# Two edits to the order of work in a hybrid attention block: pinned splits of the mixed heads, and six filling steps ahead of each first score

## The chip, the core and the metric

The kernel runs on one core of one Trainium2 chip. Its metric is the device time of one execution, in microseconds (us). TensorE (PE in the profile) multiplies; VectorE (DVE) and ScalarE (ACT) work on its results and prepare its operands; GpSimd (POOL) issues some of the DMA transfers, SyncE (SP) most of the others. Each engine takes its instructions in the order of its own program and waits at the first whose inputs or buffers are not ready.

## What is computed

One residual block on a sequence of 512 tokens of 2048 columns, in float32:

```python
def hybrid_layer(x, cos, sin, pre_norm_w, w_in, q_norm_w, w_q_up, kv_norm_w, w_kv_up, w_out, post_norm_w):
    h = rms_norm(x, pre_norm_w)
    sb_q, sb_k, sb_v, sb_gate, c_q, c_kv, k_rope, mla_gate = jnp.split(h @ w_in, split_pts, axis=-1)
    o_a = from_heads(stick_breaking_attention(to_heads(sb_q, 8), to_heads(sb_k, 8), to_heads(sb_v, 8)))
    ...
    o_b = from_heads(chunk_causal_softmax_attention(q_mla, k_mla, v_mla.transpose(0, 2, 1, 3)))
    mixed = jnp.concatenate([o_a * jax.nn.silu(sb_gate), o_b * jax.nn.silu(mla_gate)], axis=-1)
    y = mixed @ w_out
    return x + rms_norm(y, post_norm_w)
```

Both attentions have 8 heads of 128 columns. In the stick-breaking one a score row goes through two sigmoids, a running product from the right, and a multiplication; the row that comes out weighs the values.

## The kernel before

**Products in three parts.** Every float32 operand is split into a high part (an ACT copy to the float32r type, line 96) and a low part (a DVE subtraction, line 99), by `split`. A product is three matmuls (`mm3`, line 127): high by high, high by low, low by high. A tile is 128 partitions by 512 columns unless it says otherwise.

**Two streams on TensorE.** Ahead of the attention and inside it, one generator, `filler` (line 635), yields the large products one step at a time; a step is one `mm3`, three matmuls of 512 columns for nearly all. In its order: the rest of the input projection, the gates of the softmax heads, then for each stick-breaking head `q`, `k` and `gate` (16 steps each; and ahead of heads 0 and 4 the values of four heads, 64 steps), then two column groups of the output product (`out_group`, 64 steps each), then the last columns. `fill(n)` takes n steps. The attention of the heads is written between such calls, so that TensorE has a filling step to do while ACT and DVE work on a head.

**A stick-breaking head** (lines 921 to 954) takes steps until its `k` and `q` are there (`need`), then `fill(4)`, then for each block b of 128 queries the scores `z` (one `mm3`; 256, 256, 384 and 512 columns), the mask, the sigmoids, the product, and 1, 3, 3 and 7 filling steps; then for each of four blocks of keys the transposes `tp`, their split `th`/`tl`, `fill(3)`, and the product with the values, `av`. The gated result `mix` goes to DRAM (`mixed[i]`, line 794, on POOL's queue). Ahead of the scores `k` is scaled (`kr`, DVE) and split (`kh` on ACT, `kl` on DVE).

**The mixed heads.** The output product needs the 16 mixed heads split again. `split_mixed` (line 381) loads one from DRAM (`mx`, POOL's queue, line 392) and splits it into `mxh` and `mxl`; `out_group(0)` calls it four times at its start and then once for each of the 16 products of 128 rows (line 447). Its order is the softmax heads 8 to 15, then 0 to 7. Later, `load_pair` and `first_sums` (lines 486 to 500) load the mixed heads again in eight pairs, one pair for each of eight pieces of weights, and DVE makes three sums of 256 columns of each pair (lines 494 to 496), each of them split once more (`s12h`, `s4`, and so on). All these loads go through one pool of four buffers, the tag `mv`, and so do the loads of `late_sums` (line 502, first operation at line 508): a load waits until the last reader of the buffer that it takes over is done.

**What sets the order.** A scheduler orders each engine's instructions by priority and by its own idea of when each is ready; it may move an instruction ahead of others that were written earlier. `tc.keep_in_program_order` takes this freedom from an instruction. All matmuls, SP's loads and the sums of weights are pinned so. The two instructions of `split` are not, except the ACT one where a caller gives `pin=True` (only the first head's small weights do).

**The end of an output group.** `out_piece` (line 411) squares and sums a finished bank on ACT (line 407, `junk`) and multiplies it by the norm's weight on DVE (line 416, `y`). The four banks of a group are the four of the tag `ps`, so the next group's first matmul waits for the first of these multiplications.

Of the kernel before, what the change touches and what calls it, by code (L numbers as in the profile page):

```python
# [10 lines left out]
F32 = mybir.dt.float32  # L11
# [4 lines left out]
ALU = mybir.AluOpType  # L16
# [41 lines left out]
def block(ctx: ExitStack, tc: tile.TileContext, a: dict):  # L58
    nc = tc.nc
    act, dve, pool, pe = nc.scalar, nc.vector, nc.gpsimd, nc.tensor  # L60
# [8 lines left out]
    def g(name, dt=F32, tag="g"):  # L69
        return gen.tile([P, S], dt, tag=tag, name=name, bufs=SLOTS[tag])  # L70
# [4 lines left out]
    def zbank(name, dt=F32):  # L75
        return psum.tile([P, S], dt, tag="z", name=name, bufs=2)
# [13 lines left out]
    def tokens(t, b):  # L90
        return t[:, b * P:(b + 1) * P]


    def split(hi, lo, src, scale=None, pin=False):
        if scale is None:
            i = act.copy(out=hi, in_=src)  # L96
            if pin:
                tc.keep_in_program_order(i)
            dve.tensor_tensor(out=lo, in0=src, in1=hi.bitcast(F32), op=ALU.subtract)  # L99
        else:  # L100
            act.activation(out=hi, in_=src, func=AF.Copy, scale=scale)
            dve.scalar_tensor_tensor(out=lo, in0=src, scalar=scale, in1=hi.bitcast(F32), op0=ALU.mult, op1=ALU.subtract)

    def weights(src, n):
        raw = ring.tile([P, 1024], F32, tag="raw", name="raw", bufs=N_RAW)
        load(out=raw[:, :n], in_=src)
        hi = ring.tile([P, 1024], F32R, tag="whi", name="whi", bufs=N_HI)
        lo = ring.tile([P, 1024], F32R, tag="wlo", name="wlo", bufs=N_HI)
        split(hi[:, :n], lo[:, :n], raw[:, :n])
        return hi, lo  # L110

    def small_weights(src, n, pin=False):
        raw = ring.tile([P, 768], F32, tag="mraw", name="mraw", bufs=1)
        pool.dma_start(out=raw[:, :n], in_=src)
        hi = ring.tile([P, 768], F32R, tag="mhi", name="mhi", bufs=1)
        lo = ring.tile([P, 768], F32R, tag="mlo", name="mlo", bufs=1)
        split(hi[:, :n], lo[:, :n], raw[:, :n], pin=pin)
        return hi, lo
# [8 lines left out]
    def mm3(out, sth, stl, mvh, mvl, first, last, **kw):  # L127
        mm(out, sth, mvh, first, False, **kw)
        mm(out, sth, mvl, False, False, **kw)
        mm(out, stl, mvh, False, last, **kw)  # L130
# [41 lines left out]
    def load_h(k, cuts=(slice(0, S),)):  # L172
        xk = g(f"xt{k}")
        hi, lo = g(f"hh{k}", F32R), g(f"hl{k}", F32R)
        hh.append(hi)
        hl.append(lo)
        for c in cuts:
            load(out=xk[:, c], in_=a["xt"][k][:, c])
            split(hi[:, c], lo[:, c], xk[:, c], scale=pre_w[:, k:k + 1])
            yield  # L180
# [200 lines left out]
    def split_mixed():  # L381
        n = len(msplit)
        if n == 2 * H:
            return
        i = order[n]
        tag = "qrt" if n < 4 else "g"
        hi, lo = g(f"mxh{i}", F32R, tag), g(f"mxl{i}", F32R, tag)
        if i == H - 1:
            mx = last_mixed[0]
        else:  # L390
            mx = g("mx", tag="mv")
            pool.dma_start(out=mx, in_=mixed[i])
        split(hi, lo, mx)
        msplit.append((hi, lo))

    def out_mm(ps, b, c, wh, wl):
# [36 lines left out]
    def out_group(gi):  # L433
        banks = [bank(f"y{b}") for b in range(NB)]
        for i in range(8):
            wh, wl = weights(a["w_o"][gi, i], 1024)
            if i == 0:
                for _ in range(4):
                    split_mixed()
            at = 8 * gi + i - 6  # L440
            if 0 <= at + 1 < H:
                load_pair(at + 1)
            if 0 <= at < H:
                first_sums(at)
            for j in range(2):
                s_ = slice(j * S, (j + 1) * S)
                split_mixed()
                for b in range(NB):
                    out_mm(banks[b], b, i * 2 + j, wh[:, s_], wl[:, s_])
                    yield  # L450
        pw = post_weight(gi)
        for b in range(NB):
            out_piece(b, gi * S, banks[b], pw)
# [9 lines left out]
    def load_weight_parts(j):  # L463
        i, c = j // 2, slice((j % 2) * S, (j % 2 + 1) * S)
        w_parts[j] = []
        for gi, k in ((2, 0), (3, 0), (3, 4), (2, 4)):
            t = g("wsum", tag="qrt")
            tc.keep_in_program_order(pool.dma_start(out=t, in_=a["w_o"][gi, k + i][:, c]))
            w_parts[j].append(t)

    def weight_sums(j):

        i, c = j // 2, slice((j % 2) * S, (j % 2 + 1) * S)
        b11, b12, b22, b21 = w_parts.pop(j)
        for n, (out, x, y) in ((0, (b11, b12, b11)), (2, (b12, b22, b12)), (1, (b22, b22, b11)), (3, (b21, b21, b22))):
            tc.keep_in_program_order(dve.tensor_tensor(out=out, in0=x, in1=y, op=ALU.subtract))
            tc.keep_in_program_order(pool.dma_start(out=w_sums[n][i][:, c], in_=out))
# [176 lines left out]
    def fill(n):  # L654
        for _ in range(n):
            next(steps, None)
        taken[0] += n

    def need(*key):
        while key not in done:  # L660
            fill(1)
        return done[key]
# [95 lines left out]
    def row_tiles(name):  # L758

        t0, t1, t2 = (g(name, tag="row") for _ in range(3))  # L760
        return [t0[:, 384:], t1[:, :256], t0[:, :384], t2]
# [31 lines left out]
    def put_aside(i, t):  # L793
        pool.dma_start(out=mixed[i], in_=t)
# [126 lines left out]
    for h in range(H):  # L921
        if h == 0:
            fill(8)
            weight_sums(H - 1)
        kh, kl = need("k", h)
        qh, ql = need("q", h)
        fill(4)
        rows = row_tiles("beta")
        if h < H - 1:
            load_weight_parts(h)  # L930
        for b in range(NB):
            n = (b + 1) * P
            w = max(n, 256)
            z = zbank("z")
            mm3(z[:, :w], tokens(qh, b), tokens(ql, b), kh[:, :w], kl[:, :w], True, True)
            dve.tensor_tensor(out=z[:, n - P:n], in0=z[:, n - P:n], in1=m_sb, op=ALU.add)
            keep, prod, beta = g("keep", tag="tr"), g("prod", tag="tr"), rows[b]
            act.activation(out=keep[:, :n], in_=z[:, :n], func=AF.Sigmoid, scale=rq_neg[:, b:b + 1])
            act.activation(out=beta, in_=z[:, :n], func=AF.Sigmoid, scale=rq_pos[:, b:b + 1])
            dve.tensor_tensor_scan(out=prod[:, :n][:, ::-1], data0=keep[:, :n][:, ::-1], data1=zero.broadcast_to([P, n]),  # L940
                                   initial=1.0, op0=ALU.mult, op1=ALU.add)
            dve.tensor_tensor(out=beta[:, :n - 1], in0=beta[:, :n - 1], in1=prod[:, 1:n], op=ALU.mult)
            fill((1, 3, 3, 7)[b])
        if h < H - 1:
            weight_sums(h)
        cur = Weighted(rows, need("v", h // 4), (h % 4) * P)
        for j in range(NB):
            cur.turn(j)
            fill(3)
            cur.add(j)  # L950
        out = cur.finish(need("gate", h))
        if h == H - 1:
            last_mixed[0] = out
        put_aside(h, out)
# [58 lines left out]
```

## Time and profile before

| | us |
|---|---|
| median of 3 runs | 852.88 (852.85 to 853.16) |
| the profiled execution: device time | 851.63 |
| its span, first to last instruction | 849.9 |
| PE busy | 834.2, 98% of the span |
| DVE, ACT, POOL busy | 484.5, 361.6, 90.2 |

TensorE is the bound: nearly all of the chain that ended last is PE. Its busy time overstates the work a little, since a matmul's end is modelled and overlaps the next one's start. So a wait of TensorE is best read from the starts in the timeline: matmuls of 512 columns that follow each other without a wait start 0.227 us apart, and what lies beyond that is lost. The largest such losses behind the first 120 us lie in one place of head 6 of the stick-breaking heads and at the start of the second output group.

### The profile page before, as it was taken

Reading aid. Unit: us, or ns where it says so; the run is one execution under the profiler, and the core shown is the slowest. Engines: PE = TensorE matmul, PEld = TensorE weight load, DVE = VectorE, ACT = ScalarE, POOL = GpSimd, SP = SyncE. Lnnn points to the kernel's source line nnn. Section 1 sums busy time; section 2 is a strip of 40 time slices with the busy share of each in tenths; the row PEclk is TensorE's granted clock in tenths of the full one; section 3 lists DMA queues with packets and bytes.
Section 4 is the critical chain, followed back from the end, with each engine's and each line's share of the span. In section 5 each row is a group of like instructions: output and inputs, shape, how many; then the busy total and the mean of one; then the engine's idle time right before and its main releaser. Section 6 shows DMA issues by size and latency. Waiting matters only on the chain.

```text
span 849.9 us, 10987 instructions
## 1 busy us (share of the span) xinstructions
PE 834.2 (98%) x4050; PEld 700.0 (82%) x4050; DVE 484.5 (57%) x866; ACT 361.6 (43%) x620; POOL 90.2 (11%) x189
## 2 busy tenths in 40 slices
PE   8999999999999999999999999999999999999995
PEld 5889988888888888888888888888878888888884
DVE  5676765556665533647374623555574768435876
ACT  7742655545555323334242413333342535324641
POOL 1000000000000040111111010111120122100001
PEclk9999999999999999999999999999999999999999
DMA  9823222222221164434434342425362556525984
GB/s 333 342 81 106 100 81 81 81 94 81 81 90 65 63 223 161 146 99 164 161 124 154 131 140 97 145 91 199 131 222 98 179 176 222 162 99 182 324 305 155
DMA packets 41909, 126.84 MB, mean 149 GB/s; under 512 B 5808, under 2 KB 6080, under 8 KB 41856
## 3 DMA queue, kind: packets, MB, share of 16 engines
q1 hardware_dynamic: 29952, 88.62, 30.0%
q0 software_dynamic: 10608, 35.42, 12.6%
q10 hardware_dynamic: 1296, 2.11, 0.7%
q8 instruction: 32, 0.52, 0.3%
q14 instruction: 21, 0.17, 0.1%
HBM read 109.34 MB, written 16.78 MB: 148 GB/s over the span
## 4 chain that ended last, share of the span: by engine, by line
PE 87%; DMA 4%; DVE 3%; issue 3%; ACT 1%; POOL 1%; SPq 0%; DVEq 0%; POOLq 0%; ACTq 0%
PE gps L122 19%; PE v L122 10%; PE qp L122 10%; PE kp L122 9%; PE y L122 6%; PE cq L122 4%; PE av L122 4%; PE mz L122 3%; DMA mx<-mixed 3%; PE mqp L122 3%; PE sx L122 3%; PE sz L122 3%; PE ckv L122 2%; PE sv L122 2%; PE tp L125 2%
## 5 line engine op out<-in xcount | busy, mean ns | idle before, releaser
L99 DVE TENSOR_TENSOR wlo<-raw,whi 128x1024 fp32r<-128x1024 f32 (+2 forms) x137 | 163.2, 1191 | 138.6 <-ACT whi L96 137.1
L96 ACT CAST whi<-raw 128x1024 fp32r<-128x1024 f32 (+2 forms) x137 | 140.6, 1026 | 212.5 <-PE v L122 43.5
L122 PE MATMUL gps<-hh,whi 128*128 128x512 f32 x256 | 102.0, 398 | 0.0
L122 PE MATMUL gps<-hl,whi 128*128 128x512 f32 x256 | 100.1, 391 | 0.0
L122 PE MATMUL gps<-hh,wlo 128*128 128x512 f32 x256 | 99.9, 390 | 0.0
L122 PEld LDWEIGHTS gps<-hh,wlo 128*128 128x128 f32 x256 | 48.1, 188 | 10.6
L99 DVE TENSOR_TENSOR tl<-tp,th 128x512 fp32r<-128x512 f32 (+1 forms) x64 | 31.1, 486 | 42.4 <-ACT th L96 42.0
L96 ACT CAST th<-tp 128x512 fp32r<-128x512 f32 (+1 forms) x64 | 27.1, 424 | 66.2 <-PE tp L125 66.0
L122 PEld LDWEIGHTS gps<-hl,whi 128*128 128x128 f32 x256 | 48.3, 189 | 7.6
L122 PEld LDWEIGHTS gps<-hh,whi 128*128 128x128 f32 x256 | 48.2, 188 | 7.6
L122 PE MATMUL qp<-hh,whi 128*128 128x512 f32 x128 | 52.1, 407 | 0.0
L122 PE MATMUL v<-whi,hh 128*128 128x512 f32 x128 | 50.9, 397 | 0.0
L122 PE MATMUL y<-whi,mxh 128*128 128x512 f32 x128 | 50.3, 393 | 0.2 <-DVE y L416 0.2
L122 PE MATMUL qp<-hh,wlo 128*128 128x512 f32 x128 | 50.1, 391 | 0.0
L122 PE MATMUL qp<-hl,whi 128*128 128x512 f32 x128 | 50.0, 391 | 0.0
L122 PE MATMUL v<-whi,hl 128*128 128x512 f32 x128 | 49.9, 390 | 0.0
L122 PE MATMUL v<-wlo,hh 128*128 128x512 f32 x128 | 49.9, 390 | 0.0
L122 PE MATMUL y<-whi,mxl 128*128 128x512 f32 x128 | 49.9, 390 | 0.0
L122 PE MATMUL y<-wlo,mxh 128*128 128x512 f32 x128 | 49.9, 389 | 0.0
L122 PE MATMUL kp<-hh,whi 128*128 128x512 f32 x128 | 49.8, 389 | 0.0
L122 PE MATMUL kp<-hl,whi 128*128 128x512 f32 x128 | 49.8, 389 | 0.0
L122 PE MATMUL kp<-hh,wlo 128*128 128x512 f32 x128 | 49.8, 389 | 0.0
(296 smaller groups left out, 1790.6 us busy)
## 6 DMA issues: line engine op xcount, KB each, us to landing
raw<-in_w_t SPq DMA_DIRECT2D x64, 512.0 KB, 3.3
raw<-in_w_o SPq DMA_DIRECT2D x24, 512.0 KB, 3.3
mx<-mixed POOLq DMA_DIRECT2D x39, 256.0 KB, 3.5
raw<-in_w_v SPq DMA_DIRECT2D x16, 512.0 KB, 3.2
wsum<-in_w_o POOLq DMA_DIRECT2D x32, 256.0 KB, 5.2
w_sums<-wsum POOLq DMA_DIRECT2D x32, 256.0 KB, 2.6
raw<-w_sums SPq DMA_DIRECT2D x16, 512.0 KB, 3.4
xs<-in_x SPq DMA_DIRECT2D x16, 256.0 KB, 6.3
```

Of the source, the lines that this page charges most:

```text
L96: i = act.copy(out=hi, in_=src)
L99: dve.tensor_tensor(out=lo, in0=src, in1=hi.bitcast(F32), op=ALU.subtract)
L122: tc.keep_in_program_order(pe.matmul(out=out, lhsT=lhsT, rhs=rhs, start=start, stop=stop, **kw))
L125: tc.keep_in_program_order(pe.transpose(out, in_, identity))
```

## The change

`split` pins both of its instructions where it is told to, and `split_mixed` tells it to. So the 16 pairs of `mxh` and `mxl` stay where they are written, and neither is moved ahead. And a stick-breaking head takes six filling steps, not four, ahead of its first scores. No instruction is added or removed.

```diff
@@ -94,9 +94,10 @@
     def split(hi, lo, src, scale=None, pin=False):
         if scale is None:
             i = act.copy(out=hi, in_=src)
+            j = dve.tensor_tensor(out=lo, in0=src, in1=hi.bitcast(F32), op=ALU.subtract)
             if pin:
                 tc.keep_in_program_order(i)
-            dve.tensor_tensor(out=lo, in0=src, in1=hi.bitcast(F32), op=ALU.subtract)
+                tc.keep_in_program_order(j)
@@ -390,7 +391,7 @@
         else:
             mx = g("mx", tag="mv")
             pool.dma_start(out=mx, in_=mixed[i])
-        split(hi, lo, mx)
+        split(hi, lo, mx, pin=True)
         msplit.append((hi, lo))
@@ -924,7 +925,7 @@
         kh, kl = need("k", h)
         qh, ql = need("q", h)
-        fill(4)
+        fill(6)
         rows = row_tiles("beta")
```

On TensorE the matmuls are the same in both kernels; in each head two filling steps (six matmuls) move from behind the fourth scores to ahead of the first, and so the `gate` of a head is done two steps after its fourth scores and not four. The first place where the order of other engines changes much is ACT in head 6. `kh` is the high part of that head's keys, `whi` that of a piece of weights, `mxh` that of a mixed head. Before:

```order
L96 CAST qh<-qp 128x512
L96 CAST mxh_6050<-mx 128x512
L96 CAST mxh_6056<-mx 128x512
L96 CAST whi<-raw 128x1024
L96 CAST mxh_6074<-mx 128x512
L96 CAST mxh_6101<-mx 128x512
L96 CAST whi<-raw 128x1024
L96 CAST mxh_6137<-mx 128x512
L96 CAST kh<-kr 128x512
L96 CAST mxh_6176<-mx 128x512
```

After:

```order
L96 CAST qh<-qp 128x512
L96 CAST whi<-raw 128x1024 x2
L96 CAST kh<-kr 128x512
L96 CAST whi<-raw 128x1024
L939 ACTIVATE keep<-z,rq_neg 128x128
L940 ACTIVATE beta<-z,rq_pos 128x128
```

No mixed head is split in head 6 any more: all are split in head 7 and behind it. One cast of a mixed head stands ahead of that head's `kh`, the next three right behind it, and three more between the sigmoids of its four blocks, the fifth mixed head's between those of the first and of the second. The second place is POOL's queue, where the loads for the splits end and those for the pairs begin (`mixed_1224` and `mixed_1225` are mixed heads 6 and 7, 1218 to 1223 the heads 0 to 5, 1226 is mixed head 8; L392 and L393 load for `split_mixed`, L481 and L482 for the pairs, L794 and L795 write a head's result). Before:

```order
L392 DMA mx<-mixed_1219 128x512
L392 DMA mx<-mixed_1220 128x512
L392 DMA mx<-mixed_1221 128x512
L775 MEMSET th 128x128
L776 MEMSET tl 128x128
L794 DMA mixed_1224<-mix 128x512
L392 DMA mx<-mixed_1222 128x512
L392 DMA mx<-mixed_1223 128x512
L481 DMA mx<-mixed_1226 128x512
L481 DMA mx<-mixed_1218 128x512
```

After:

```order
L393 DMA mx<-mixed_1219 128x512
L393 DMA mx<-mixed_1220 128x512
L776 MEMSET th 128x128
L777 MEMSET tl 128x128
L393 DMA mx<-mixed_1221 128x512
L393 DMA mx<-mixed_1222 128x512
L795 DMA mixed_1225<-mix 128x512
L393 DMA mx<-mixed_1223 128x512
L482 DMA mx<-mixed_1226 128x512
L482 DMA mx<-mixed_1218 128x512
```

The same loads stand a whole head later: the first pair's two loads (1226 and 1218) came ahead of the write of mixed head 7 and now come behind it, with one load for the splits (1223, mixed head 5) between. The third place is DVE ahead of the first output group's multiplications (`y`); `st` are the sums of a pair, 6721 being the third sum of the eighth and last pair, and L508 and L509 the first operations of `late_sums`. Before:

```order
L494 TENSOR_TENSOR st<-mx 128x256
L508 TENSOR_TENSOR mx<-mx 128x256
L495 TENSOR_TENSOR st<-st,mx 128x256
L496 TENSOR_TENSOR st_6721<-mx,st 128x256
L508 TENSOR_TENSOR mx<-mx 128x256
L99 TENSOR_TENSOR s12l<-st,s12h 128x512
L99 TENSOR_TENSOR s_6727<-st_6721,s_6727 128x256
L99 TENSOR_TENSOR wlo<-raw,whi 128x1024
L508 TENSOR_TENSOR mx<-mx 128x256 x2
L99 TENSOR_TENSOR wlo<-raw,whi 128x1024
L416 TENSOR_TENSOR y_6466<-y_6040,pw 128x512
```

After:

```order
L495 TENSOR_TENSOR st<-mx 128x256
L496 TENSOR_TENSOR st<-st,mx 128x256
L97 TENSOR_TENSOR wlo<-raw,whi 128x1024
L497 TENSOR_TENSOR st_6721<-mx,st 128x256
L97 TENSOR_TENSOR s12l<-st,s12h 128x512
L97 TENSOR_TENSOR s_6727<-st_6721,s_6727 128x256
L509 TENSOR_TENSOR mx<-mx 128x256
L417 TENSOR_TENSOR y_6466<-y_6040,pw 128x512
```

In both kernels all eight pairs of sums stand ahead of the first `y` on DVE, and on ACT their splits stand ahead of its square. Of the loads for `late_sums` one is left ahead of it, not four; a `wlo` now stands between the second and the third sum of the last pair.

## Rows read from the trace of the kernel before

**Rows 1.** The page: busy time of all engines, and the group of weight casts.

```profile
PE 834.2 (98%) x4050; PEld 700.0 (82%) x4050; DVE 484.5 (57%) x866; ACT 361.6 (43%) x620; POOL 90.2 (11%) x189
...
L96 ACT CAST whi<-raw 128x1024 fp32r<-128x1024 f32 (+2 forms) x137 | 140.6, 1026 | 212.5 <-PE v L122 43.5
```

**Rows 2.** Timeline of PE, head 6: start, duration, instruction, [idle before <-releaser].

```profile
622.73 0.39 PE L122 MATMUL gps<-hl,whi 128*128 128x512 f32 x1
622.96 0.39 PE L122 MATMUL gps<-hh,wlo 128*128 128x512 f32 x1
624.63 0.39 PE L122 MATMUL z<-kh,qh 128*128 128x256 f32 x1 [1.28 <-ACT kh L96]
625.35 0.39 PE L122 MATMUL z<-kl,qh 128*128 128x256 f32 x1 [0.34 <-DVE kl L99]
...
639.35 0.39 PE L122 MATMUL av<-th,vh 128*128 128x512 f32 x1
640.04 0.50 PE L122 MATMUL av<-tl,vh 128*128 128x512 f32 x1 [0.30 <-DVE tl L99]
```

**Rows 3.** Timeline of ACT, head 6.

```profile
623.44 0.62 ACT L96 CAST mxh<-mx 128x512 fp32r<-128x512 f32 x1 [2.37 <-DMA mx<-mixed]
623.96 0.61 ACT L96 CAST kh<-kr 128x512 fp32r<-128x512 f32 x1
```

**Rows 4.** Timeline of DVE and of PE in head 5.

```profile
584.21 0.68 DVE L99 TENSOR_TENSOR kl<-kr,kh 128x512 fp32r<-128x512 f32 x1
...
585.52 0.28 PE L122 MATMUL z<-kl,qh 128*128 128x256 f32 x1
```

**Rows 5.** Timeline of DVE and of PE in head 7: last beta, first transposes.

```profile
673.68 0.69 DVE L942 TENSOR_TENSOR beta<-beta,prod 128x511 f32<-128x511 f32 x1
...
675.20 0.60 PE L125 MATMUL tp<-ident,beta 128*128 128x128 f32 x4
```

**Rows 6.** Timeline of PE where the second output group starts.

```profile
719.77 0.39 PE L122 MATMUL y<-whi,mxl 128*128 128x512 f32 x1
720.39 0.50 PE L122 MATMUL y<-whi,mxh 128*128 128x512 f32 x1 [0.23 <-DVE y L416]
```

**Rows 7.** Timeline of DVE from head 7's result to the group's end.

```profile
686.85 0.69 DVE L790 TENSOR_TENSOR mix<-av,gt 128x512 f32<-128x512 f32 x1 [1.77 <-PE av L122]
687.46 0.41 DVE L494 TENSOR_TENSOR st<-mx 128x256 f32<-128x256 f32 x1
...
712.07 0.43 DVE L508 TENSOR_TENSOR mx<-mx 128x256 f32<-128x256 f32 x1 [1.74 <-DMA mx<-mixed]
...
718.51 1.22 DVE L99 TENSOR_TENSOR wlo<-raw,whi 128x1024 fp32r<-128x1024 f32 x1
719.65 0.68 DVE L416 TENSOR_TENSOR y<-y,pw 128x512 f32<-128x512 f32 x1
```

**Rows 8.** Timeline of ACT, the last pair's last cast and the first square.

```profile
713.39 0.40 ACT L96 CAST s<-st 128x256 fp32r<-128x256 f32 x1
...
718.16 0.58 ACT L407 ACTIVATE junk<-y 128x512 f32<-128x512 f32 x1 [2.30 <-PE y L122]
718.65 0.19 ACT L407 ACTIVATION_READ_ACCUMULATOR junk<-y 128x1 f32 x1
```

**Rows 9.** Timeline of POOL: head 7's write, and the first load after a pair's sums.

```profile
687.84 0.54 POOL L794 DMA_DIRECT2D mixed<-mix  x1 [5.90 <-DVE mix L790]
688.63 0.55 POOL L481 DMA_DIRECT2D mx<-mixed  x1 [0.24 <-DVE st L495]
```

**Rows 10.** Loads of mx issued in 688 to 709 us: count, and time to landing.

```profile
L481 POOL DMA_DIRECT2D mx<-mixed x14: 546/546/548, 688.6 to 708.3; - x14
...
DMA to landing us min/median/max: 2.9/3.9/5.6
```

**Rows 11.** The same for the loads issued in 720 to 735 us.

```profile
L481 POOL DMA_DIRECT2D mx<-mixed x4: 546/547/548, 724.4 to 732.6; - x4
...
DMA to landing us min/median/max: 2.8/3.4/3.8
```

**Rows 12.** The same for the loads issued in 664 to 680 us.

```profile
L392 POOL DMA_DIRECT2D mx<-mixed x3: 546/546/548, 664.3 to 671.4; - x3
...
DMA to landing us min/median/max: 2.8/3.0/4.3
```

## The prediction, made before the changed kernel had run

> **What bounds the kernel now.** I read the page first: PE is busy for 98% of the span [rows 1], so only what keeps PE from its next matmul can move the time, and no instruction is added or removed. I then went through PE's timeline by the starts: matmuls of 512 columns without a wait start 0.227 us apart (622.73 and 622.96 in [rows 2]), so a larger step is a loss of the difference. In the part that the change reorders there are two such places. The first is head 6: 622.96 to 624.63 is 1.67, a loss of 1.44; 624.63 to 625.35 is 0.72 behind a matmul of 256 columns (half of 0.227), a loss of 0.61; 639.35 to 640.04 loses 0.46. Together **2.51 us**. The second is the start of the second output group: 719.77 to 720.39 loses 0.39 [rows 6]. The reader should see what released each wait: the high part of the keys (`kh`), on ACT, and that cast stood behind the cast of a mixed head which itself waited 2.37 us for its load [rows 3]. A head without mixed splits has no such wait: in head 5 `kl` ends at 584.89 and is wanted at 585.52 [rows 4].
>
> **Part one: head 6.** With no `mxh` on ACT and no `mxl` on DVE in head 6, its chain `kr`, `kh`, `kl` is that of head 5, and with the two added steps it has 0.63 + 2 x 3 x 0.227 = 2.0 us to spare. The wait for `tl` goes too, since it came from DVE running late behind the same splits. Gain: 2.51, nearly certain. Each edit alone would do most of it (six matmuls are 1.36 us of the 2.05 at the scores, pinning takes away all of it).
>
> **Part two: six steps in the other heads.** They had no wait to lose, so the gain is nothing. Two steps move ahead of the scores, and the transposes stay where they are in PE's order or later, so ACT and DVE lose no time either. One thing gets closer: the gate's bank must be read by DVE before the fourth later step wants it (head 3, where the second values begin, and head 7, where the output begins). Followed through the new order DVE is done 0.1 us ahead in both. I take nothing; the other end is one DVE operation of 512 columns, 0.69 like that for `mix` [rows 7], at each.
>
> **Part three: head 7's transposes.** ACT now has the fifth mixed head's cast between the sigmoids of the first and the second block. Its load takes over the first one's buffer, so it goes out at about 664 on the clock of before, and everything behind that cast on ACT and on DVE (masks, sigmoids, running products) waits for it. Followed op by op, the last `beta` is done at 673.4 plus the load's time L. The transposes want it at 675.20 + 1.36 = 676.56; before, it was done at 674.37 [rows 5]. With L of 3.0, the middle of the loads issued about there [rows 12], nothing is lost; with 4.3 it is 1.1. I take 0.2.
>
> **Part four: the pairs, and the end of the first output group.** This is the term that decides. On DVE and ACT all eight pairs of sums stand ahead of the first group's square and multiplication, which free the bank that PE wants next. Before, the first pair's loads went out in head 7 and its sums began at 687.46 [rows 7]; the last pair's last cast ended at 713.79 and the square began at 718.16, when PE had delivered [rows 8]: 4.4 us to spare. (The 0.39 lost there came from a `wlo` of 1.22 ahead of `y` [rows 7], which has moved forward.)
>
> After, the loads of the pairs stand behind those of the splits, in the same four buffers. Head 7's `mix` comes at 686.85 + 1.36 (two steps) + 0.2 = 688.4. POOL writes it 0.99 after its start [rows 7, 9], and only behind that may the load of mixed head 5 go: at 690.0. It lands at 690.0 + L. Then come its cast (0.62, as in [rows 3]), a weight cast (1.03 in the mean [rows 1]) and that weight's subtraction (1.22 [rows 7]), in ACT's and DVE's order ahead of the first sums, which so begin at about 692.8 + L. The second pair is no longer loaded ahead: its second load takes the buffer of the first pair's first tile, going out 1.17 after the first sums began, as the load at 688.63 did [rows 7, 9]. From there one load leads to the next but one pair: after landing two sums (0.88), a `wlo` in between (1.15 to the next start), the third sum (0.43), 0.3 to the issue, and L again. That is 2.8 + L for two pairs, three times to the eighth; then the same sums and the last casts (2.9 with its hand-over). So the last cast ends at 692.8 + L + 1.17 + L + 3 x (2.8 + L) + 2.9, about 705.3 + 5L. The square (0.58 and 0.19 [rows 8]), `y` (0.68 [rows 7]) and hand-overs (0.15) make it 706.9 + 5L when PE may go on. PE would be ready at 720.39 - 0.39 + 0.2 = 720.2.
>
> **L** is the load's time to landing. In the stretch of the pairs the 14 loads, in twos, took 2.9 to 5.6, the middle one 3.9 [rows 10]; four loads issued singly took 2.8 to 3.8, in the middle 3.4 [rows 11]. The chain's loads go singly, but each shortly behind a load of weights, which the end of the `wlo` lets go. I take 3.65, between the two middles. Then PE goes on at 725.15, 4.76 later than before. As a check without the chain: the eight pairs took 713.79 - 687.46 = 26.3 before, one of them loaded ahead, with a wait of 1.74 for a load that now stands elsewhere [rows 7, 8]; 696.45 + 26.3 plus the same 1.6 is 724.4.
>
> The Trainium skill, page "DMA: Bandwidth & Descriptors", section "Anatomy of one DMA — SWDGE (gpsimd) path", fits a load from POOL's queue as 2.0 us plus its bytes at 436 GB/s, which for 256 KB makes 2.6 us as an estimate. By that rule the pairs would keep up and the time would be 850.2. The trace does not agree for this stretch: no load in [rows 10] took under 2.9.
>
> **The sum.** +4.76 - 2.51 = **+2.25 us**. On the profiled execution that is 849.9 to 852.15 of span; its device time is 851.63, 1.25 under the median of the runs, so I add the difference to the median: 852.88 + 2.25 = **855.1**. Every 0.1 us of L moves it by 0.5: L of 2.8, 3.4, 3.9 and 4.3 give 850.9, 853.9, 856.4 and 858.4.
>
> **The rivals.** (1) Faster: the pairs keep up. If L is below 2.66, 706.9 + 5L is under 720.2, nothing is lost at the second group, not the old 0.39 either: -2.51 - 0.39 + 0.2 = -2.7, 850.2. For it: single loads of 2.8 do occur [rows 11, 12]; and my chain may start too late by a microsecond or two, which does the same. Against: five loads in a row would all have to be that fast. Above 0.2% it decides from L of 2.87. (2) Within 0.2%: L between 2.87 and 3.54, where what the pairs cost and what head 6 gives about cancel; 851.2 to 854.6. For it, the median of [rows 11]. (3) Much slower: the loads meet those of the weights each time and take 4.3 or more: 858.4 and up; head 7's transposes then lose up to 1.1 of it. (4) The pinning does nothing: excluded, the instructions' order shows the splits moved.
>
> **How the numbers follow.** About 0.2%, 1.7 us, is what a measurement of this kernel can tell from no change: 851.2 to 854.6. The forecast (855.1, L of 3.55 to 4.3) has 0.42 and rival 3 has 0.08, both slower; rival 2 has 0.33; rival 1 has 0.17, faster. The range leaves out the ends of rivals 1 and 3: 850.6 to 858.4.
>
> **What would show it.** Right: in head 6 PE's `z` and `av` follow without a wait; the first sums on DVE begin 8 to 10 us later against the start of `y` than before; ACT's first square waits for DVE or a load and not for PE; PE has one wait of 3 to 6 us for `y` at the start of the second group. Wrong: no such wait there, the first sums earlier than 5 us behind those of before, or loads of `mx` in that stretch under 3 us; or a wait of PE that I took as nothing, at the fourth step of a bank or for `beta` in head 7.

## The result: slower, and by more than forecast

| | us |
|---|---|
| changed kernel, median of 4 runs | 860.32 (859.34 to 861.04) |
| kernel before, beside it, 4 runs | 852.87 |
| ratio, 95% interval | 1.0089 (1.0073 to 1.0104) |
| the profiled execution: device time, span | 859.34, 857.5 |

The direction was right. The size was not: 7.45 us lost where 2.25 were forecast, and the time lies above the range. The profiled span grew by 7.6 us, from 849.9 to 857.5.

The page of the changed kernel, its busy times [rows 1 for before], says little: the same instructions, a busy share of PE as high as before.

```profile
PE 836.6 (98%) x4050; PEld 702.2 (82%) x4050; DVE 487.4 (57%) x866; ACT 360.3 (42%) x620; POOL 90.1 (11%) x189
```

What PE waited for says more. In the list of its waits (engine, line, who was waited for, us in total, times, longest) `kh`, `kl` and `tl` are gone, and `y` heads it:

```profile
PE y L123 <- DVE y L417: 6.7, 1, 6.7
```

PE's timeline (start, duration, instruction, idle before) shows what is new by the starts: losses in head 0 and at head 3's second values, the scores of head 6, which now follow without a wait [rows 2], and losses in head 7 and at the start of the second output group:

```profile
357.14 0.39 PE L123 MATMUL gps<-hh,wlo 128*128 128x512 f32 x1
358.02 0.44 PE L123 MATMUL z<-kh,qh 128*128 128x384 f32 x1 [0.49 <-ACT beta L940]
...
477.92 0.39 PE L123 MATMUL v<-whi,hl 128*128 128x512 f32 x1
478.67 0.50 PE L123 MATMUL v<-whi,hh 128*128 128x512 f32 x1 [0.37 <-DVE gt L345]
...
625.31 0.39 PE L123 MATMUL gps<-hh,wlo 128*128 128x512 f32 x1
625.53 0.28 PE L123 MATMUL z<-kh,qh 128*128 128x256 f32 x1
...
674.89 0.49 PE L126 MATMUL tp<-ident,beta 128*128 128x128 f32 x3
675.65 0.33 PE L126 MATMUL tp<-ident,beta 128*128 128x128 f32 x1 [0.28 <-DVE beta L943]
675.74 0.47 PE L123 MATMUL y<-whi,mxh 128*128 128x512 f32 x1
...
718.45 0.39 PE L123 MATMUL y<-whi,mxl 128*128 128x512 f32 x1
725.54 0.80 PE L123 MATMUL y<-whi,mxh 128*128 128x512 f32 x1 [6.71 <-DVE y L417]
726.13 0.63 PE L123 MATMUL y<-wlo,mxh 128*128 128x512 f32 x1
...
730.77 0.39 PE L123 MATMUL y<-whi,mxh 128*128 128x512 f32 x1
```

Against a step of 0.227 the start at 725.54 lost 6.86 (before, 0.39 [rows 6]). And the loss doesn't end there: from 725.54 to 730.77 the 12 steps took 5.23 us where 12 x 0.227 is 2.72. **2.51 us** went to matmuls that ran at half speed. The row of the clock says why (stretch, its length, busy us and count of PE, PEld, DVE, ACT and POOL, then PEclk, the granted clock as a share of full speed, the DMA engines' busy share, and GB/s):

```profile
715.00:724.00 9.00, 3.83 (x17) 2.83 (x16) 8.18 (x16) 3.87 (x8) 2.81 (x6) 0.99 0.72 230
724.00:731.00 7.00, 5.46 (x13) 4.37 (x14) 5.08 (x10) 3.76 (x11) 0.45 (x1) 0.52 0.54 199
```

After a stretch in which PE stood idle, the granted clock was at its lower level, 1.2 GHz, for most of 724 to 731. In the kernel before it is 1.00 in both stretches.

The balance, by the starts: head 6 gives 2.51; the start of the second group costs 6.86 - 0.39 = 6.47 more than before; the clock 2.51; head 0 0.65 and head 3 0.52 (steps of 0.88 and 0.75, less 0.227), head 7 0.50 (its four transposes take 0.85 from the first start, 674.89, to that of the next product, 675.74, and 0.35 in the other heads). Together +8.1. The changed kernel's attention began 0.37 us earlier: the `mz`, a product of the softmax attention, that waits 0.69 us in both kernels stands at 119.72 and not at 120.09. That is not put down to the change, since in the profiled runs of the experiments it stands anywhere from 119.55 to 122.87. That makes +7.8, against 7.6 of span. One loss is larger than the old 0.39 at the second group and stays out of the balance, since it is the same in both kernels: 0.54 where the last columns begin (`sv`), at 808.14 before and at 815.65 after.

Why the wait is long is to be seen on DVE and ACT. The rows are the first sums of pairs one, two, four and eight, then the last pair's last cast, the square, and the multiplication that frees PE's bank:

```profile
695.01 0.42 DVE L495 TENSOR_TENSOR st<-mx 128x256 f32<-128x256 f32 x1
699.26 0.43 DVE L495 TENSOR_TENSOR st<-mx 128x256 f32<-128x256 f32 x1 [0.78 <-DMA mx<-mixed]
708.60 0.42 DVE L495 TENSOR_TENSOR st<-mx 128x256 f32<-128x256 f32 x1 [3.53 <-DMA mx<-mixed]
721.26 0.43 DVE L495 TENSOR_TENSOR st<-mx 128x256 f32<-128x256 f32 x1 [0.39 <-DMA mx<-mixed]
...
723.65 0.41 ACT L96 CAST s<-st 128x256 fp32r<-128x256 f32 x1 [0.85 <-DVE st L497]
723.96 0.58 ACT L408 ACTIVATE junk<-y 128x512 f32<-128x512 f32 x1
...
724.80 2.48 DVE L417 TENSOR_TENSOR y<-y,pw 128x512 f32<-128x512 f32 x4
```

The steps are those foretold (a load, two sums, a `wlo`, the third sum, the next load), with one that is longer than the others: 702 to 708.6. The load that it waited for (count, duration in ns, first and last start; then the time to landing):

```profile
L482 POOL DMA_DIRECT2D mx<-mixed x1: 546/546/546, 701.9 to 701.9; - x1
...
DMA to landing us min/median/max: 6.6/6.6/6.6
```

And the timeline of SP's queue in that stretch (SPq: issues of DMAs, first start and time to the last of the group):

```profile
698.18 0.33 SPq L88 DMA_DIRECT2D pw<-in_post_w  x1
698.56 30.55 SPq L88 DMA_DIRECT2D raw<-in_w_o  x7
```

That load took 6.6 us. The five loads of the chain took 3.5 (from 688.71 to its cast at 692.26), 3.0, 6.6, 3.7 and 3.4. Ahead of the long one no load of weights had left SP's queue since 680.4; at 698.18 the group's norm weight `pw` went out, and right behind it three loads of weights, at 698.56, 699.03 and 701.32. So there were two guesses to test: that the pairs' chain makes the wait and the wait makes the slow clock, and that SP's burst makes the long load.

### The profile page after: what moved, and what is told of

It is laid out like the page before. It is cut to its first block, busy times and chain, and to the rows that moved or that the text cites. A ratio compares the mean times of both kernels' runs of the same rounds, so it can differ in the third digit from the quotient of the medians.

```text
span 857.5 us, 10989 instructions
## 1 busy us (share of the span) xinstructions
PE 836.6 (98%) x4050; PEld 702.2 (82%) x4050; DVE 487.4 (57%) x866; ACT 360.3 (42%) x620; POOL 90.1 (11%) x189
## 4 chain that ended last, share of the span: by engine, by line
PE 85%; issue 5%; DVE 4%; DMA 3%; ACT 2%; POOL 1%; SPq 0%; DVEq 0%; POOLq 0%; ACTq 0%
PE gps L123 17%; PE qp L123 10%; PE v L123 10%; PE kp L123 9%; PE y L123 6%; PE cq L123 4%; PE av L123 4%; PE mz L123 3%; PE mqp L123 3%; PE sz L123 3%; PE ckv L123 2%; PE sv L123 2%; PE tp L126 2%; PE sx L123 2%; DMA mx<-mixed 2%
```

## Experiments

Each ratio is against runs of the kernel before beside it; those differed a little between the sittings (medians of 851.45 to 853.07), so ratios are compared, and spans within a trace's own terms. A ratio can differ by 0.001 from that of the two medians.

### Each edit alone

The pinning alone is the changed kernel with

```diff
-        fill(6)
+        fill(4)
```

> The pinning alone, with four filling steps as before. Theory: the pinning makes the loss. It takes the pairs of sums behind the splits, and PE waits for the first y of the first output group; the wait makes the granted clock fall for some microseconds behind it. So here too PE should wait 6 to 10 us for y (on DVE four operations of the late sums stand ahead of y here, in the changed kernel one, so rather more than its 6.7), and the clock falls to 1.2 GHz behind it. The waits of 0.65 in head 0 and 0.53 ahead of head 3's second values should be gone, since they come from the six steps. Head 6 waits for nothing or for a few tenths. Time 858 to 863. Rival: the six steps are the cause, since they push the gate and head 7 later: then the time is 850 to 852 and PE waits under 2 us for y.

Measured: 860.73, ratio 1.0106 (1.0092 to 1.012). From PE's timeline:

```profile
623.17 0.28 PE L123 MATMUL z<-kh,qh 128*128 128x256 f32 x1
...
717.17 0.39 PE L123 MATMUL y<-whi,mxl 128*128 128x512 f32 x1
726.08 0.80 PE L123 MATMUL y<-whi,mxh 128*128 128x512 f32 x1 [8.52 <-DVE y L417]
```

The whole loss is here, without the six steps: the start of the second group costs 8.68 - 0.39 = 8.29 more than before, the eight slow steps behind it (726.08 to 729.61) 1.71, and head 6 gives 2.51, which makes +7.5, against 7.6 of span. Head 6's scores follow without a wait (no bracket). The waits in heads 0 and 3 are absent. The wait for `y` is longer than in the changed kernel (8.52 and 6.71), as expected with four operations of the late sums ahead of it.

The six steps alone are the kernel before with

```diff
-        fill(4)
+        fill(6)
```

> Six filling steps alone, nothing of the mixed heads pinned. Theory: no long wait for y (the pairs stand where they stood before), no fall of the clock there. Head 6 gains the two steps, 1.36 us of its 2.05 at the scores, and keeps or loses a part of the 0.46 at av; head 0 and head 3 lose 0.65 and 0.53 as in the changed kernel. Sum: 852.87 - 1.36 + 1.18, and up to 0.46 less: 852.2 to 852.7. Rival: the long wait belongs to the six steps: 857 or more.

Measured: 854.98, ratio 1.0053 (1.0034 to 1.0072). One of the five runs took 859.02; the ratio of the medians is 1.0041. Both theories missed the whole. There is no long wait for `y` (a loss of 0.82 at 723.78), and head 0 and head 3 lose 0.64 and 0.52 as expected; but head 7's output lost 0.50 for the gate's bank (at 678.18), and head 6, which should have gained, lost. The timeline of ACT and PE there:

```profile
633.41 0.62 ACT L96 CAST mxh<-mx 128x512 fp32r<-128x512 f32 x1 [1.55 <-DMA w_sums<-wsum]
...
639.93 0.34 PE L125 MATMUL tp<-ident,beta 128*128 128x128 f32 x1 [1.91 <-DVE beta L942]
640.02 0.68 PE L122 MATMUL qp<-hh,whi 128*128 128x512 f32 x1
```

And the row of the clock for the stretch behind:

```profile
640.00:645.00 5.00, 5.00 (x17) 3.97 (x18) 2.42 (x4) 1.64 (x2) 0.00 (x0) 0.66 0.35 115
```

With the unpinned splits still in head 6, the casts of mixed heads stand between the sigmoids of its blocks, and one waits there 1.55 us, for the write of a sum of weights (`w_sums`) whose buffer it takes over; their subtractions stand between the masks and products on DVE. The transposes then wait 1.91 us for the last `beta`. The wait at the scores has only moved, and it also took the clock down (granted 0.66 in 640 to 645, 1.00 in 635 to 640). So the six steps buy nothing by themselves; what frees head 6 is the pinning.

### The pairs, put back behind the group's end

Here the three sums of a pair are pinned, and their splits, in the changed kernel:

```diff
-        dve.tensor_tensor(out=s1, in0=x[:, HALF:], in1=y[:, HALF:], op=ALU.add)
+        tc.keep_in_program_order(dve.tensor_tensor(out=s1, in0=x[:, HALF:], in1=y[:, HALF:], op=ALU.add))
...
-        split(h12, l12, t)
+        split(h12, l12, t, pin=True)
```

(and so for `s2`, `s4` and the second split). As written, four pairs come ahead of the first group's `y`, not eight.

> The changed kernel, with the three sums of each pair and their splits pinned too. In DVE's and ACT's order four pairs now stand ahead of the first group's squares and multiplications, and four behind them, as they are written. Nothing else ahead of that place moves much. Theory: the wait for y is the chain of eight pairs, and the low clock is its consequence; with four pairs the last of them is done some 7 us ahead of PE, so both go: 860.3 - 6.9 - 2.5 = 850.9, between 850.3 and 851.5, and the granted clock stays at 2.4 GHz through the change of groups. Rival: the four pairs behind y only carry the wait on to the end of the second group or to the product that reads their sums; then a wait of 3 us or more stands there and the time is 854 to 860. Second rival: the low clock isn't the wait's doing but that of the place: then it falls without the wait, and the time is 853.4.

Measured: 850.48, ratio 0.9988 (0.9979 to 0.9997), a difference to the changed kernel of 1.0% or 8.6 us. PE's timeline at the change of groups:

```profile
718.43 0.39 PE L123 MATMUL y<-whi,mxl 128*128 128x512 f32 x1
718.66 0.44 PE L123 MATMUL y<-whi,mxh 128*128 128x512 f32 x1
```

And the clock behind it:

```profile
724.00:731.00 7.00, 7.00 (x33) 5.79 (x32) 4.19 (x9) 3.04 (x4) 1.39 (x3) 1.00 0.80 245
```

No wait and no slow matmul; even the old 0.39 is gone. The four later pairs carry no wait on: nothing new stands behind this place.

The same kernel with four steps ahead of the scores:

> As the one before, with four filling steps ahead of a head's scores and not six. Theory: the waits of 0.65 (head 0, scores, for beta) and 0.53 (head 3, second values, for the gate) in the changed kernel come from the two steps, and pinning alone keeps head 6 free: so this is 1.2 less than the one before, 849.7, between 849.3 and 850.5, and both waits are absent. Rival: with four steps head 6 has a wait of 0.3 or more for kh again, or the two waits have another cause: 850.5 to 851.5.

Measured: 848.69, ratio **0.9969 (0.9958 to 0.998)**. It beats both kernels. The time is 0.6 under the range expected; its span is 1.5 us under that of the run before it (846.8 and 848.3), where 1.2 was expected, and neither of the two small waits is there. ACT in head 0 shows where the first came from. With six steps (the kernel above):

```profile
355.28 1.05 ACT L96 CAST whi<-raw 128x1024 fp32r<-128x1024 f32 x1 [4.28 <-issue]
356.36 1.28 ACT L939 ACT_TABLE_LOAD   x1
```

And with four, where the first sigmoid follows at 354.13:

```profile
351.23 1.28 ACT L939 ACT_TABLE_LOAD   x1
```

With six steps a cast of weights stands between `kh` and the first sigmoid, and the table load, which otherwise is done while ACT has nothing to do, comes behind that cast. So the cast's 1.05 and the table load's 1.28 us lie on the way to the first sigmoids, at 357.65, and to the `beta` that frees the bank of the third scores. Whether one of the two alone would make the wait was not tried.

### The clock by itself

The changed kernel with matmuls in the wait, into a bank that nothing reads:

```diff
-        pw = post_weight(gi)
+        pw = post_weight(gi); [mm(wb, tokens(msplit[0][0], 0), wh[:, :S], True, True) for wb in ([tbank("warm")] if gi == 0 else []) for _ in range(26)]
```

> The changed kernel, with 26 matmuls of 512 columns into a spare bank written between the two output groups; nothing reads what they make. They take 26 x 0.227 = 5.9 us of the 6.9 in which PE waits for y in the changed kernel; the order of the other engines ahead of that place is the same. Theory: the matmuls at 0.427 behind the wait come from PE's idleness. Then the granted clock stays at 2.4 GHz, the wait for y that is left is 0.8 to 1.2 us, and the run is 2.5 us shorter than the changed kernel, against before a ratio of 1.006 and not 1.009. Rival: the low clock belongs to the place, or to the load of the DMA engines there: then it falls all the same, and the time is that of the changed kernel or more.

Measured: 858.23, ratio 1.0062 (1.0044 to 1.0081); span 855.3. PE's timeline:

```profile
718.82 6.05 PE L123 MATMUL warm<-whi,mxh 128*128 128x512 f32 x26
725.58 0.50 PE L123 MATMUL y<-whi,mxh 128*128 128x512 f32 x1 [0.70 <-DVE y L417]
725.92 0.39 PE L123 MATMUL y<-wlo,mxh 128*128 128x512 f32 x1
```

And the row of the clock:

```profile
724.00:731.00 7.00, 6.30 (x28) 4.86 (x27) 5.88 (x12) 3.85 (x11) 0.98 (x2) 1.00 0.39 147
```

The second group begins at the same time (725.58 and 725.54), since what it waits for is unchanged, but at full speed. So the low clock is the idleness's doing, not that of the place. Nor is it that of the DMAs: behind the same place their busy share was 0.80 at a granted 1.00 with the pairs put back, and 0.54 at 0.52 in the changed kernel. The intervals of this ratio and of the changed kernel's overlap; the verdict rests on the trace, where the 2.5 us are simply absent.

### The load that took 6.6 us

First the size. Half of each load for the pairs is left out (columns 256 to 511; the sums read the other half twice), and the first group's squares, multiplications and the late sums are pinned:

```diff
-    pairs = {}
+    pairs, mixed_half = {}, lambda n: [t := g("mx", tag="mv"), pool.dma_start(out=t[:, :HALF], in_=mixed[order[n]][:, :HALF])][0]
...
-        pairs[j] = mixed_again(j), mixed_again(j + 8)
+        pairs[j] = mixed_half(j), mixed_half(j + 8)
...
-        dve.tensor_tensor(out=s1, in0=x[:, HALF:], in1=y[:, HALF:], op=ALU.add)
+        dve.tensor_tensor(out=s1, in0=x[:, :HALF], in1=y[:, :HALF], op=ALU.add)
```

> The changed kernel, with half of each load for the pairs of sums left out: 128x256 and not 128x512, and the sums read the half that is there twice. The first group's squares and multiplications and the late sums are pinned, so that as in the changed kernel at most one late sum stands ahead of the first y; on DVE the third sum of every second pair now stands ahead of a weight's subtraction and not behind it, which takes up to 3 x 1.15 us out of the chain of loads. Theory: the wait for y is a chain of loads one behind the other (3.5, 3.0, 6.6, 3.7 and 3.5 us in the changed kernel, 20.3 in all), the one of 6.6 in a stretch in which the DMA engines are full. With half the bytes the pairs' loads take 2.3 to 3.3, the one of 6.6 under 4.5, so at least 4 us go from the chain beside the 3.5; the wait for y is under 1 us and the clock stays. Rival: it is the work of DVE and ACT on eight pairs and the weights that fills the stretch; then more than 3 us of wait stay.

Measured: 857.27, ratio 1.0051 (1.0033 to 1.007). The theory fell in part. The loads of 128 KB issued at 698.9 to 700.1 took 2.3 us; but behind SP's burst, which in this run began at 700.8, they took as long as those of 256 KB had:

```profile
L485 POOL DMA_DIRECT2D mx<-mixed x2: 546/546/546, 702.5 to 703.1; - x2
...
DMA to landing us min/median/max: 6.3/6.4/6.5
```

The timeline of DVE and PE:

```profile
709.64 0.43 DVE L495 TENSOR_TENSOR st<-mx 128x256 f32<-128x256 f32 x1 [3.63 <-DMA mx<-mixed]
...
725.68 0.73 PE L123 MATMUL y<-whi,mxh 128*128 128x512 f32 x1 [3.98 <-DVE y L417]
```

DVE still waited 3.63 us for one load, and PE 3.98 for `y`. After that load the first sums of a later pair wait for DMA by 0.28 at most, so there the work of DVE and ACT itself sets the pace, and nothing behind it makes up for the 3.63: the rival was half right. And the long load isn't long by its own bytes.

Then the burst. The first group's norm weight goes to a buffer that is free early (the order of instructions is the same on every engine):

```diff
-        pw = post_weight(gi)
+        pw = post_weight(gi, "t" if gi == 0 else "tr")
```

> The changed kernel, with the first group's norm weight (pw) loaded into a buffer of another tag, which is free early; the order of instructions is that of the changed kernel on every engine. There pw waited on SP's queue until 698.2 us for a buffer that the first pair's sums hold, and three loads of weights (512 KB each) left at 698.6, 699.0 and 701.3, at once behind it. Theory: these 1.75 MB fill the DMA engines, and the pairs' loads issued at 700 to 704 take 5.5 to 6.7 us for that, the one on the chain 6.6. Without the wait of pw the weights' loads leave one by one from about 689 on, the load on the chain takes 3 to 4 us, and the wait for y falls from 6.9 by 2.5 to 3.5 us, to 3.4 to 4.4. Against before the ratio is 1.0055 if the clock still falls behind the wait, 1.0025 if it doesn't. Rival: the pairs' own four loads in a row make it (with half the bytes one still took 6.5, which speaks against it): then nothing changes, 1.009.

Measured: 858.77, ratio 1.0063 (1.0042 to 1.0084). SP's queue:

```profile
684.46 0.33 SPq L88 DMA_DIRECT2D pw<-in_post_w  x1
689.57 37.84 SPq L88 DMA_DIRECT2D raw<-in_w_o  x7
```

The pairs' loads issued in 698 to 706 us:

```profile
L482 POOL DMA_DIRECT2D mx<-mixed x5: 546/548/548, 697.6 to 704.9; - x5
...
DMA to landing us min/median/max: 3.0/3.4/4.0
```

PE's timeline, and then the clock of the stretch behind:

```profile
718.68 0.39 PE L123 MATMUL y<-whi,mxl 128*128 128x512 f32 x1
723.85 0.80 PE L123 MATMUL y<-whi,mxh 128*128 128x512 f32 x1 [4.79 <-DVE y L417]
...
728.97 0.40 PE L123 MATMUL y<-whi,mxh 128*128 128x512 f32 x1
```

```profile
724.00:731.00 7.00, 7.00 (x21) 5.60 (x22) 4.16 (x8) 2.11 (x6) 0.55 (x1) 0.66 0.40 137
```

With the weights' loads spread, no load of a pair in this stretch takes over 4.0, and the wait loses 1.9 us (6.86 to 4.94 by the starts), somewhat less than the 2.5 to 3.5 expected. The pairs' loads still follow each other as in the changed kernel, so the rival, that they make the long load themselves, falls; the busy share of the DMA engines from 698 to 708 is 0.68 here and 0.92 there. The clock falls behind 4.79 us of waiting as well: the 12 steps from 723.85 to 728.97 take 5.12 us, 2.40 more than at full speed. This ratio's interval too overlaps that of the changed kernel, and the verdict rests on the trace.

## Why the prediction was right in direction and wrong in size

**Part one, head 6:** right for the change as a whole, all 2.51 us. Its remark that each edit alone would do most of it was right of the pinning, which does all of it, and wrong of the six steps, which do none (they turn the wait at the scores into one at the transposes).

**Part two, six steps elsewhere:** taken at nothing, it cost 1.17. The wait at head 3's second values is the near tie that was named, and went the wrong way, as one of the prediction's own signs of being wrong: 0.52, within the bound of 0.69; the other of the two places lost nothing of its own. Head 0's 0.65 was not seen at all. The step that failed is "ACT and DVE lose no time either": it looked at PE's order, while on ACT two steps let a cast of weights, and with it a table load, in ahead of the first sigmoid.

**Part three, head 7's transposes:** 0.50 where 0.2 was taken; a small term, right in kind.

**Part four, the pairs:** the mechanism was right, and so was the working where its L held. Of its 4.76, 0.2 are part three's delay, which moves the chain and PE alike; the place itself was forecast at 725.15 - 720.2 - 0.39 = 4.56 more than before. The last run tells: there the chain's five loads took 3.2, 3.8, 4.0, 3.8 and 3.6, together 18.4 where 5 x 3.65 = 18.25 was taken, and the place costs 4.94 - 0.39 = 4.55 more. What was mis-sized is L itself: in the changed kernel the five loads took 20.2, by one load of 6.6. The middles of [rows 10] and [rows 11] could not show that. But [rows 10] did hold loads of 5.5 and 5.6, and I had not asked what was issued beside them. In the kernel before, SP's queue and the two loads are:

```profile
691.59 0.33 SPq L88 DMA_DIRECT2D pw<-in_post_w  x1
...
L481 POOL DMA_DIRECT2D mx<-mixed x2: 546/546/546, 692.5 to 693.1; - x2
...
DMA to landing us min/median/max: 5.5/5.6/5.6
```

So there too the slowest loads went out just behind `pw` (and one load of weights, at 691.97); those issued from 699.9 to 702.5 took 2.9 to 3.1. `pw` waits for a buffer of the tag that the first pair's sums take, so moving those sums later also moved SP's whole queue later, and let it go at once, onto a load of the chain. SP's queue was not followed, and that is the lesson of this term: 1.91 us (6.47 - 4.56).

**What was missing altogether** is the term that weighs most: 2.51 us of matmuls at 1.2 GHz behind the wait. The sum priced a wait of five microseconds at five microseconds. The Trainium skill, page "TensorE: Matmul & The Clock Gate", section "HAM oscillation — how this bites in real kernels", says of a kernel whose matmuls wait for their data between bursts that such a wait throttles the clock, so that each next burst starts slow. The traces here agree: 0.52 granted behind 6.71 us of waiting, 1.00 when matmuls fill it.

Together: 1.91 + 2.51 + 1.17 + 0.30 = 5.9 us over the forecast; measured 5.2 by the medians (7.45 - 2.25). The earlier start is 0.37 of the difference; the other 0.3 is not traced.

**The rivals:** the third, much slower by slow loads, came closest: the mean of the chain's loads was 4.04, between its 4.3 and the forecast's 3.65. The measured time lies in its stretch (858.4 and up), but not for its reason: by the working an L of 4.04 gives 857.1, and one load of the five was slow, not each; it is the clock, which no rival had, that takes the time past 858.4. The estimate by the Trainium skill, page "DMA: Bandwidth & Descriptors", section "Anatomy of one DMA — SWDGE (gpsimd) path", 2.6 us for such a load, was met by none of the chain's five, which took 3.0 or more.

## What to carry to other kernels

Pinning one set of instructions lets others, still free, pile up on the near side of what they should stand behind; here the cure was to pin the pairs' sums as well, and then four filling steps are better than six (0.9969). When work moves, follow every queue that shares a buffer with it, those of other engines too. And price a wait of TensorE with what follows it: behind the five waits of 1.91 to 8.52 us here, the matmuls at half the clock cost another 1.6 to 2.5 us, and not more behind the longer ones.

## What the runs showed of the hardware

- TensorE's clock: behind waits of 8.52, 6.71, 4.79, 3.98 and, in head 6 with six steps alone, 1.91 us, matmuls of 512 columns then started 0.43 us apart for some microseconds (granted 0.52 to 0.76 in the stretches of 5 to 7 us behind them). What that cost beyond 0.227 a step is, in the order of these waits, 1.7, 2.5, 2.4, 1.7 and 1.6 us. Behind the 1.28 and 0.34 us of head 6 in the kernel before [rows 2], and behind 0.70 us with matmuls ahead of it, they did not.
- The first two loads from POOL's queue behind a burst on SP's queue (`pw` and then two or three loads of weights, 1.25 to 1.75 MB) took 6.3 to 6.7 us, whether they were of 256 or of 128 KB; the next two took 5.5 to 5.6 and 4.4 to 4.6. Ahead of the burst they took 3.0 to 3.1 (issued at 696.2 and 696.7 in the changed kernel) and 2.3. How the engines share the two queues was not tried.
